# A decoder trunk on one core: chunk 3 of x1 on ScalarE, a unit's splits ahead of the second half's norm, and block 0 of the last norm on VectorE

## The chip, the core and the metric

The kernel runs on one core of a Trainium2 chip. A core has TensorE for matrix products (PE; its weight loads are shown as PEld), VectorE (DVE), ScalarE (ACT), GpSimd (POOL) and SyncE (SP), which here only issues transfers. Each engine works through its own list of instructions in order and waits on semaphores for the others. PE writes into PSUM; DVE and ACT read PSUM and SBUF. Transfers between HBM and SBUF run on 16 DMA engines, whoever issues them.

The metric is device time in microseconds (us) of one execution; lower is better. The kernel before took 1002.99 us, the median of three runs (1001.86 to 1003.0).

## The reference

The input is a sequence of 256 tokens of width 2048. Two layers follow, each closed by `x <- LayerNorm(alpha * x + mixer(x))`, in float32:

- a Mamba-2 SSD mixer (input projection 2048 to 10304, a short convolution, the chunked state-space product, a gate, a group norm, output projection 4096 to 2048);
- a sliding-window attention mixer with sinks (32 query heads, 4 key/value heads of 64). Keys and values come from the first layer's output by one shared projection of 2048 to 512; queries and gate come from another of 2048 to 4096; an output projection of 2048 to 2048 ends it.

What the change touches is the LayerNorm after the first layer, whose result is called x1 here, the K/V projection behind it, and the LayerNorm after the second layer, whose result is the output:

```
def _layernorm(x, g, b):
    mu = mean(x); var = mean((x - mu)^2)
    return (x - mu) * rsqrt(var + EPS) * g + b
kv = x1 @ kv_w + kv_b
```

## The kernel before

**Split products.** Every large product is made of three, to keep float32 accuracy: each operand is split into a high half (ACT copies it to a reduced float32, tile `wh` for weights, L158) and a low half (DVE subtracts the high half from the original, tile `wl`, L161), and PE adds high x high, low x high and high x low. x1 is split likewise into `x1H` (L893, one of them L891 on DVE) and `x1L` (L894).

**Units.** Weights come in units of 128 x 2048. `load_next` (L219) loads a unit as two 512 KB transfers on SP into the rotating raw tiles `wr` and splits both halves (`split_half`, L152). `next_unit` (L231) hands out the next unit and sees to it that two more are loaded behind it (`AHEAD = 2`). There are four buffers each of `wh` and `wl` and six of `wr`.

**Order.** The program order of each engine is set by a scheduler from dependences and priorities; instructions marked with `keep_in_program_order` (the arguments `pin`, `pin_h`, and the helper `ordered` in the last norm) keep the order in which the code writes them.

**Between the layers.** The rows are two halves (h) of 128 tokens; a chunk or block (c, nb) is 512 of the 2048 columns. L900 to L908 run the last output products of the first layer in the order (0,0), (1,0), (0,1), (0,2), (0,3), (1,1), (1,2), (1,3) of (h, nb), add the result to `xr` (L312) and take each block's statistics (L843). Behind a half's last block, `center(h)` (L860) makes mean (L847), scale `rs` (L849, L850, ACT) and `nmr` (L864), and centres and scales the half: chunks 0 and 2 on DVE (L870), 1 and 3 on ACT (L868). `turn_x1(h, c)` (L872) then transposes a chunk on PE (L877), applies the norm's g and b from PSUM in four pieces of 128 (even chunks on ACT, L887; odd ones on DVE, L885) and splits it.

**K/V.** L955 to L963: for h = 0, four units are taken one after the other; `x_stat` (L936) makes twelve matmuls of 512 columns for each (L944). The argument `last` puts one of the three products of a unit at its end. Behind the third unit, the four chunks of the second half are transposed. For h = 1 the same four units are used again.

**The last norm.** `out_last` (L316) makes the last output products, and `behind` (L1216) takes statistics; behind the last piece of the second half, `last` (L1194) runs. It makes mean and scale, a diagonal matrix `dg` of the scale on ACT (L1202), and centres the four blocks on DVE (`centre`, L1175, times g). Then some pieces get scale and bias on PE (identity x b, L1199, then `dg` x the centred piece, L1208) and are copied to `xr` by ACT (L1209); the others get them on DVE (`scale`, L1182). `store` (L1171) issues the output transfers, on SP unless another engine is named.

Of the kernel before, what the change touches and what calls it, by code (L numbers as in the profile page):

```python
# [27 lines left out]
AHEAD = 2  # L28
# [54 lines left out]
def trunk(ctx: ExitStack, tc: tile.TileContext, A: dict, out: bass.AP, dbg=None):  # L83
    nc = tc.nc
# [49 lines left out]
    WHOLE = [(0, 0, KT)]  # L134
# [17 lines left out]
    def split_half(u, raw, c, pin=False, pin_h=False):  # L152
        for (h, k0, k1), (l, _, _) in zip(*u.parts):
            a, b = max(k0, 8 * c), min(k1, 8 * c + 8)
            if a < b:
                sl = slice((a - k0) * P, (b - k0) * P)
                v = raw[:, (a - 8 * c) * P : (b - 8 * c) * P]
                m = nc.scalar.activation(h[:, sl], v, AF.Copy)  # L158
                if pin_h:
                    tc.keep_in_program_order(m)  # L160
                m = nc.vector.tensor_tensor(l[:, sl], v, h[:, sl].bitcast(F32), ALU.subtract)  # L161
                if pin:
                    tc.keep_in_program_order(m)

    def load_unit(src, places, pin=False):
        u = new_unit(places)
        raws = [load_half(u, src, c) for c in range(2)]
        for c in range(2):
            split_half(u, raws[c], c, pin, pin)
        return u  # L170

    def load_first():
# [24 lines left out]
    srcs = []  # L197
# [12 lines left out]
    places = {}  # L210
# [5 lines left out]
    units = []  # L216
    used = [0]

    def load_next(n, pin=False):  # L219
        for _ in range(n):  # L220
            if len(units) == 4:
                nc.sync.dma_start(cc[:], A["cc"])
            for i in [i for i, n in enumerate(XK_AT) if n == len(units)]:

                v = xr[:, i % 2, i // 2 * 1024 : i // 2 * 1024 + 1024]
                tc.keep_in_program_order(
                    nc.sync.dma_start(v, A["xk"][:, i % 2, i // 2 * 1024 : i // 2 * 1024 + 1024])
                )
            units.append(load_unit(srcs[len(units)], places.get(len(units), [WHOLE, WHOLE]), pin))

    def next_unit():  # L231
        load_next(min(used[0] + 1 + AHEAD, len(srcs)) - len(units))
        used[0] += 1
        return units[used[0] - 1]

# [29 lines left out]
    xr = xr_t[:, : 2 * D].rearrange("p (h d) -> p h d", h=2)  # L265
# [591 lines left out]
    nc.gpsimd.dma_start(gbc[:], A["gbc"])  # L857
    st1 = lp.tile([P, 2, 4, 6], F32, tag="st", name="st1")

    def center(h):  # L860

        mv, rs = norm_scale(lp, st1, h)
        nmr = lp.tile([P, 1], F32, tag="nmr", name=nm("nmr"), bufs=2)
        nc.vector.tensor_scalar(nmr[:], mv[:, 0:1], rs[:], -1.0, ALU.mult, ALU.mult)  # L864
        for c in range(4):
            v = xr[:, h, c * 512 : (c + 1) * 512]
            if c % 2:
                nc.scalar.activation(v, v, AF.Identity, scale=rs[:], bias=nmr[:])  # L868
            else:
                nc.vector.tensor_scalar(v, v, mv[:, 0:1], rs[:], ALU.subtract, ALU.mult)  # L870

    def turn_x1(h, c, tp, tag, bufs):  # L872

        ps = ax_tile()
        for k in range(4):
            pinned(
                nc.tensor.transpose(  # L877
                    ps[:, k * P : (k + 1) * P], xr[:, h, c * 512 + k * P : c * 512 + (k + 1) * P], ident
                ), True,
            )  # L880
        x1 = tp.tile([P, 512], F32, tag=tag, name=nm("x1"), bufs=bufs)[:].rearrange("p (k t) -> p k t", k=4)
        for k in range(4):
            v, g_, b_ = ps[:, k * P : (k + 1) * P], *[gbc[:, i, c * 4 + k : c * 4 + k + 1] for i in range(2)]
            if c % 2:
                nc.vector.tensor_scalar(x1[:, k, :], v, g_, b_, ALU.mult, ALU.add)  # L885
            else:
                nc.scalar.activation(x1[:, k, :], v, AF.Identity, scale=g_, bias=b_)  # L887
        dst = (slice(None), slice(c * 4, c * 4 + 4), slice(h * P, (h + 1) * P))
        if (h, c) == (0, 0):

            nc.vector.tensor_copy(x1H[dst], x1)  # L891
        else:
            nc.scalar.activation(x1H[dst], x1, AF.Copy)  # L893
        nc.vector.tensor_tensor(x1L[dst], x1, x1H[dst].bitcast(F32), ALU.subtract)  # L894
# [5 lines left out]
    for h, nb in ((0, 0), (1, 0), (0, 1), (0, 2), (0, 3), (1, 1), (1, 2), (1, 3)):  # L900
        if h == 0:
            us[nb] = next_unit()
        out_unit(*yHL, h, us[nb], nb, False, rms, True)
        norm_stats(st1, h, nb)
        if nb == 3:
            center(h)
        for c in {(1, 2): (0, 1), (1, 3): (2, 3)}.get((h, nb), ()):
            turn_x1(0, c, x1p, "x1", 2)  # L908
    s2.close()
# [26 lines left out]
    def x_stat(ps, h, u, ui, pin=False, last=None):  # L936

        todo = [(k, i) for k in range(4) for i in range(3) if i != last]
        todo += [(k, last) for k in range(4) if last]
        for k, i in todo:  # L940
            kk = ui * 4 + k
            ks = slice(k * 512, (k + 1) * 512)
            hs = slice(h * P, (h + 1) * P)
            m = nc.tensor.matmul(  # L944
                ps[:], (x1H, x1L, x1H)[i][:, kk, hs], (u.h, u.h, u.l)[i][:, ks],
                start=(kk, i) == (0, 0), stop=ui == 3 and (k, i) == todo[-1],
            )
            pinned(m, pin)
# [5 lines left out]
    kv_u = []  # L954
    for h in range(2):  # L955
        ps = mm_tile()
        for ui in range(4):
            if h == 0:
                kv_u.append(next_unit())
            x_stat(ps, h, kv_u[ui], ui, h == 0, (1, 1, 2, None)[ui] if h == 0 else None)  # L960
            if h == 0:
                for c in ((), (), (0, 1, 2, 3), ())[ui]:
                    turn_x1(1, c, bp, "pt", NPT)  # L963
        kd = bp.tile([P, 4, 2, 64], F32, tag="qt", name=nm("kd"), bufs=2)
        nc.vector.tensor_tensor(
            kd[:, :, 0, :], ps[:, :256].rearrange("p (j d) -> p j d", j=4),
            kvb[:, :256].rearrange("p (j d) -> p j d", j=4), ALU.add,
        )
        nc.vector.tensor_tensor(vt[:, h, :], ps[:, 256:], kvb[:, 256:], ALU.add)
        rope(kd[:, :, 0, :], h, 4)  # L970
        nc.gpsimd.tensor_copy(kd[:, :, 1, :], kd[:, :, 0, :])

        def ktr(h=h, kd=kd):
            pt = ax_tile()
            for j in range(4):
                nc.tensor.transpose(
                    pt[:, j * P : (j + 1) * P], kd[:, j, :, :].rearrange("p a d -> p (a d)"), ident
                )
            nc.scalar.copy(kT[:, :, h * P : (h + 1) * P], pt[:].rearrange("p (j t) -> p j t", j=4))

        later(2, ktr)
# [185 lines left out]
    def cols(nb, c0=0, c1=512):  # L1167
        return slice(nb * 512 + c0, nb * 512 + c1)

    def store(h, sl, eng=nc.sync):  # L1170
        ordered(eng.dma_start(out[h * P : (h + 1) * P, sl], xr[:, h, sl]))  # L1171

    def centre(h, nb):
        t = bp.tile([P, 512], F32, tag="pt", name=nm("t"), bufs=NPT)
        ordered(nc.vector.scalar_tensor_tensor(  # L1175
            t[:], xr[:, h, cols(nb)], sc[h][0][:, 0:1], gb2[0][:, cols(nb)], ALU.subtract, ALU.mult
        ))
        ts[h, nb] = t

    def scale(h, nb, c0=0):  # L1180
        sl = cols(nb, c0)
        ordered(nc.vector.scalar_tensor_tensor(  # L1182
            xr[:, h, sl], ts[h, nb][:, c0:], sc[h][1][:], gb2[1][:, sl], ALU.mult, ALU.add
        ))
        store(h, sl)
# [7 lines left out]

    def last():  # L1194

        pieces = [(0, 0, 256), (0, 256, 512), (1, 0, 512), (2, 0, 256)]
        pss = [ax_tile()[:, : p[2] - p[1]] for p in pieces]
        for p, ps in zip(pieces, pss):
            ordered(nc.tensor.matmul(ps, ident, gb2[1][:, cols(*p)], start=True, stop=False))  # L1199
        sc[1] = norm_scale(bp, st2, 1, 5)  # L1200
        dg = bp.tile([P, P], F32, tag="dg", name="dg")
        ordered(nc.scalar.activation(dg[:], ident, AF.Copy, scale=sc[1][1][:]))  # L1202
        for c in range(4):
            centre(1, c)
            for p, ps in zip(pieces, pss):
                if p[0] != c:
                    continue
                ordered(nc.tensor.matmul(ps, dg[:], ts[1, c][:, p[1] : p[2]], start=False, stop=True))  # L1208
                ordered(nc.scalar.copy(xr[:, 1, cols(*p)], ps))  # L1209
                if c == 0:  # L1210
                    store(1, cols(*p))
        scale(1, 3)
        scale(1, 2, 256)
        store(1, slice(512, 1280), nc.scalar)

    def behind(h, nb, c0=0, c1=512):  # L1216
        ordered(norm_stats(st2, h, nb, c0, c1))
# [105 lines left out]
```

## Time and profile before

| what | value |
|---|---|
| median of three runs | 1002.99 us (1001.86, 1002.99, 1003.0) |
| the profiled execution | 1002.04 us, its span 1000.2 us |
| PE busy | 992.7 us, 99% of the span |
| DVE, ACT, POOL busy | 772.9, 565.8, 105.2 us |
| HBM read | 195.43 MB |
| granted TensorE clock | 1.00 of full speed |

How the lines are read: times are in us from the start of the span unless marked ns. A row of the timeline has start, length, engine, line of the kernel, operation, destination <- source, shape, a count (xN, instructions of one kind merged into one row), and in brackets how long the engine was idle before it and what it waited for. A row of waits has: engine, line and what it waited for; then total us, number of times, longest. The chain of waits is the path that ended last, followed back from the last instruction. In the DMA view, a line of GB/s gives 40 equal slices of the window, and a row of issues gives the count, KB each, and the median us from issue to landing. The queue called q14 brings instructions.

### The profile page before, as it was taken

To read this page: it belongs to the slowest core of one execution; us is meant where nothing else is said; L and a number is where in the kernel's file an instruction comes from. 1 tells how busy PE (TensorE), PEld (TensorE's weight loads), DVE (VectorE), ACT (ScalarE), POOL (GpSimd) and SP (SyncE) were. 2 spreads that over 40 slices of the span, in tenths; PEclk is the share of its full clock that TensorE was granted. 3 is DMA by queue.
4 is the path that set the end of the run, shared out by engine and by line. 5 is a ranking of instruction groups with operands and counts; after the bars stand their busy time and mean duration, and the time that the engine had idled before them with its cause. 6 is when DMAs were issued, how large, how long until landed. Compare 5 with 4: busy or idle time off the path is not lost.

```text
span 1000.2 us, 17847 instructions
## 1 busy us (share of the span) xinstructions
PE 992.7 (99%) x7040; PEld 900.3 (90%) x7040; DVE 772.9 (77%) x1189; ACT 565.8 (57%) x986; POOL 105.2 (11%) x130
## 2 busy tenths in 40 slices
PE   9999999999999999999999999999999999999997
PEld 8999989999999998999999999888988878878976
DVE  7888897867886886786786787898688775775685
ACT  7595856547746645664654764565545544544632
POOL 0001303004003003000300300303000000000003
PEclk9999999999999999999999999999999999999999
DMA  9798587565576655666656556457654546546422
GB/s 358 251 285 296 169 273 211 175 226 177 183 242 183 224 195 191 213 193 207 206 174 225 164 177 223 163 162 252 230 194 148 182 147 195 159 149 194 167 104 84
DMA packets 58963, 198.81 MB, mean 199 GB/s; under 512 B 6560, under 2 KB 10944, under 8 KB 58624
## 3 DMA queue, kind: packets, MB, share of 16 engines
q1 hardware_dynamic: 56080, 188.47, 57.8%
q0 software_dynamic: 2336, 8.69, 2.7%
q8 instruction: 55, 0.90, 0.4%
q10 hardware_dynamic: 464, 0.52, 0.1%
q14 instruction: 28, 0.23, 0.1%
HBM read 195.43 MB, written 2.23 MB: 198 GB/s over the span
## 4 chain that ended last, share of the span: by engine, by line
PE 96%; DVE 2%; ACT 1%; issue 0%; DVEq 0%; ACTq 0%
PE mm L238 52%; PE mm L944 10%; PE mm L305 9%; PE mm L307 8%; PE mm L306 8%; PE ax L605 2%; PE ax L1056 1%; PE ax L1114 1%; PE ax L581 1%; PE ax L1096 1%; ACT wh L158 1%; DVE wl L161 0%; PE mm L364 0%; PE ax L564 0%; PE ax L1019 0%
## 5 line engine op out<-in xcount | busy, mean ns | idle before, releaser
L161 DVE TENSOR_TENSOR wl<-wr,wh 128x1024 fp32r<-128x1024 f32 (+2 forms) x338 | 393.0, 1182 | 109.0 <-ACT wh L158 106.7
L158 ACT ACTIVATE wh<-wr 128x1024 fp32r<-128x1024 f32 (+2 forms) x338 | 332.7, 1011 | 208.4 <-issue 84.9
L238 PE MATMUL mm<-xH,wh 128*128 128x256 f32 x1280 | 356.0, 278 | 0.0
L238 PE MATMUL mm<-xL,wh 128*128 128x256 f32 x1280 | 354.4, 277 | 0.0
L238 PE MATMUL mm<-xH,wl 128*128 128x256 f32 x1280 | 354.3, 277 | 0.0
L238 PEld LDWEIGHTS mm<-xH,wh 128*128 128x128 f32 x1280 | 240.9, 188 | 2.1 <-issue 0.5
L238 PEld LDWEIGHTS mm<-xL,wh 128*128 128x128 f32 x1280 | 240.9, 188 | 1.0
L238 PEld LDWEIGHTS mm<-xH,wl 128*128 128x128 f32 x1280 | 240.9, 188 | 0.0
L305 PE MATMUL mm<-wh,yH 128*128 128x512 f32 x256 | 101.4, 396 | 0.0
L306 PE MATMUL mm<-wh,yL 128*128 128x512 f32 x256 | 99.8, 390 | 0.0
L307 PE MATMUL mm<-wl,yH 128*128 128x512 f32 x256 | 99.7, 389 | 0.0
L621 POOL TENSOR_TENSOR yz<-yz,z 128x256 f32<-128x256 f32 x32 | 32.8, 1032 | 472.2 <-DVE yz L616 472.2
L238 PE MATMUL mm<-x1H,wh 128*128 128x256 f32 x256 | 71.7, 280 | 0.0
L468 DVE SCALAR_TENSOR_TENSOR cv<-mm,pc,cv 128x255 f32<-128x255 f32 x144 | 68.5, 476 | 3.3 <-ACT cv L466 1.9
L238 PE MATMUL mm<-x1L,wh 128*128 128x256 f32 x256 | 70.8, 277 | 0.0
L238 PE MATMUL mm<-x1H,wl 128*128 128x256 f32 x256 | 70.8, 276 | 0.0
L944 PE MATMUL mm<-wh,x1H 128*128 128x512 f32 x160 | 62.9, 393 | 0.0
L944 PE MATMUL mm<-wl,x1H 128*128 128x512 f32 x160 | 62.1, 390 | 0.6 <-DVE wl L161 0.6
L944 PE MATMUL mm<-wh,x1L 128*128 128x512 f32 x160 | 61.3, 389 | 0.0
L305 PEld LDWEIGHTS mm<-wh,yH 128*128 128x128 f32 x256 | 48.1, 188 | 10.3 <-DVE z L557 1.0
L307 PEld LDWEIGHTS mm<-wl,yH 128*128 128x128 f32 x256 | 48.1, 188 | 10.2
L312 DVE SCALAR_TENSOR_TENSOR xr<-mm,r,xr 128x512 f32<-128x512 f32 x64 | 47.0, 743 | 12.0 <-PE mm L307 7.7
(210 smaller groups left out, 1349.7 us busy)
## 6 DMA issues: line engine op xcount, KB each, us to landing
wr<-in_wa SPq DMA_DIRECT2D x154, 512.0 KB, 4.9
wr<-in_wo SPq DMA_DIRECT2D x64, 512.0 KB, 4.4
wr<-in_wq SPq DMA_DIRECT2D x32, 512.0 KB, 4.8
wr<-in_wg SPq DMA_DIRECT2D x32, 512.0 KB, 4.7
wr<-in_wb SPq DMA_DIRECT2D x32, 512.0 KB, 4.5
rb<-rscr SPq DMA_DIRECT2D x11, 512.0 KB, 4.2
wr<-in_wkv SPq DMA_DIRECT2D x8, 512.0 KB, 5.0
first<-in_first SPq DMA_DIRECT2D x11, 352.0 KB, 6.4
```

The source lines that it names most:

```text
L158: m = nc.scalar.activation(h[:, sl], v, AF.Copy)
L161: m = nc.vector.tensor_tensor(l[:, sl], v, h[:, sl].bitcast(F32), ALU.subtract)
L238: m = nc.tensor.matmul(ps, a, b, start=first and i == 0, stop=last and i == 2)
L305: pinned(nc.tensor.matmul(ps, aH[:, k, hs], u.h[:, ks], start=k == 0, stop=False), pin)
L306: pinned(nc.tensor.matmul(ps, aL[:, k, hs], u.h[:, ks], start=False, stop=False), pin)
L307: pinned(nc.tensor.matmul(ps, aH[:, k, hs], u.l[:, ks], start=False, stop=k == 3), pin)
L312: nc.vector.scalar_tensor_tensor(v, ps, rms[:, h : h + 1], v, ALU.mult, ALU.add)
L468: nc.vector.scalar_tensor_tensor(a[:, sft:], ps[:, : S - sft], w(3 - sft), a[:, sft:], ALU.mult, ALU.add)
L581: nc.tensor.transpose(ps[:, o : o + P], st.xs[i][:, c * P : (c + 1) * P], ident)
L605: nc.tensor.matmul(ps[64 * r : 64 * r + 64, cols], xd[:, c, r, :], e[:, 256:] if c else e[:, :256], start=c == 0, stop=c == 1,)
L621: nc.gpsimd.tensor_tensor(v, v, st.z[i][:], ALU.mult)
L944: m = nc.tensor.matmul(ps[:], (x1H, x1L, x1H)[i][:, kk, hs], (u.h, u.h, u.l)[i][:, ks], start=(kk, i) == (0, 0), stop=ui == 3 and (k, i) = ...
```

## The change

1. In `turn_x1`, chunk 3 of the first half gets g and b on ACT in place of DVE.
2. `center` is divided: `center_scale` makes mean, scale and nmr; `center` does the centring. For the second half the centring is called in the K/V loop, behind the first `next_unit`, which loads the third K/V unit. The `next_unit` at ui = 1, which loads the fourth, pins the low halves' splits of its unit in program order (`pin`), not the high halves' (`pin_h`). In the compiled order on DVE, the second low half of the third unit and the low part of chunk 3 stand ahead of the second half's nmr and centring.
3. The first K/V unit of the second half multiplies by the low x (x1L) last.
4. In the last norm, DVE scales block 0 behind the second centring; blocks 1 and 2 take scale and bias on PE, block 2 in two pieces of 256; DVE scales block 3. The second half goes out in four transfers of 256 KB, three on SP and block 2's on ACT, in place of five.

```diff
-    def load_unit(src, places, pin=False):
+    def load_unit(src, places, pin=False, pin_h=False):
         u = new_unit(places)
         raws = [load_half(u, src, c) for c in range(2)]
         for c in range(2):
-            split_half(u, raws[c], c, pin, pin)
+            split_half(u, raws[c], c, pin, pin_h)
         return u
...
-    def load_next(n, pin=False):
+    def load_next(n, pin=False, pin_h=True):
...
-            units.append(load_unit(srcs[len(units)], places.get(len(units), [WHOLE, WHOLE]), pin))
-
-    def next_unit():
-        load_next(min(used[0] + 1 + AHEAD, len(srcs)) - len(units))
+            units.append(load_unit(srcs[len(units)], places.get(len(units), [WHOLE, WHOLE]), pin, pin and pin_h))
+
+    def next_unit(behind=False):
+        load_next(min(used[0] + 1 + AHEAD, len(srcs)) - len(units), behind, not behind)
         used[0] += 1
         return units[used[0] - 1]
...
-    def center(h):
-
+    def center_scale(h):
         mv, rs = norm_scale(lp, st1, h)
         nmr = lp.tile([P, 1], F32, tag="nmr", name=nm("nmr"), bufs=2)
         nc.vector.tensor_scalar(nmr[:], mv[:, 0:1], rs[:], -1.0, ALU.mult, ALU.mult)
+        return mv, rs, nmr
+
+    def center(h, mv, rs, nmr):
+
         for c in range(4):
...
-            if c % 2:
+            if c % 2 and (h, c) != (0, 3):
                 nc.vector.tensor_scalar(x1[:, k, :], v, g_, b_, ALU.mult, ALU.add)
...
         if nb == 3:
-            center(h)
+            scale1 = center_scale(h)
+            if h == 0:
+                center(h, *scale1)
...
             if h == 0:
-                kv_u.append(next_unit())
-            x_stat(ps, h, kv_u[ui], ui, h == 0, (1, 1, 2, None)[ui] if h == 0 else None)
+
+                kv_u.append(next_unit(ui == 1))
+                if ui == 0:
+                    center(1, *scale1)
+            x_stat(ps, h, kv_u[ui], ui, h == 0, ((1, 1, 2, None), (1, None, None, None))[h][ui])
...
-        pieces = [(0, 0, 256), (0, 256, 512), (1, 0, 512), (2, 0, 256)]
+        pieces = [(1, 0, 512), (2, 0, 256), (2, 256, 512)]
...
         for c in range(4):
             centre(1, c)
+            if c == 1:
+                scale(1, 0)
             for p, ps in zip(pieces, pss):
-                if p[0] != c:
-                    continue
-                ordered(nc.tensor.matmul(ps, dg[:], ts[1, c][:, p[1] : p[2]], start=False, stop=True))
-                ordered(nc.scalar.copy(xr[:, 1, cols(*p)], ps))
-                if c == 0:
-                    store(1, cols(*p))
+                if p[0] == c:
+                    ordered(nc.tensor.matmul(ps, dg[:], ts[1, c][:, p[1] : p[2]], start=False, stop=True))
+                    ordered(nc.scalar.copy(xr[:, 1, cols(*p)], ps))
+            if c in (1, 2):
+                store(1, cols(c), nc.sync if c == 1 else nc.scalar)
         scale(1, 3)
-        scale(1, 2, 256)
-        store(1, slice(512, 1280), nc.scalar)
```

## The prediction

> **What bounds the kernel.** I read the page first (busy time, the chain), then what PE waited for, then the timeline of PE, DVE and ACT around the one long wait, then the last 15 us with the DMA view.
>
> ```profile
> span 1000.2 us, 17847 instructions
> PE 992.7 (99%) x7040; PEld 900.3 (90%) x7040; DVE 772.9 (77%) x1189; ACT 565.8 (57%) x986; POOL 105.2 (11%) x130
> PE 96%; DVE 2%; ACT 1%; issue 0%; DVEq 0%; ACTq 0%
> ...
> PE ax L350 <- DVE zero L339: 1.2, 1, 1.2
> PE mm L944 <- DVE wl L161: 0.6, 1, 0.6
> ```
>
> PE is busy for 99% of the span and is 96% of the chain that ended last, so time can only leave where PE stands still or after its last matmul. The waits of PE have two rows: the start of the kernel (untouched), and one wait of a K/V matmul for a low half made on DVE. The other stretch off PE is the end, which the chain walks on DVE. The change edits exactly these two places.
>
> The place of the wait, from the timelines of PE, DVE and ACT:
>
> ```profile
> 669.22 0.39 PE L944 MATMUL mm<-wh,x1H 128*128 128x512 f32 x1
> 669.45 0.39 PE L944 MATMUL mm<-wh,x1L 128*128 128x512 f32 x1
> 671.03 0.61 PE L944 MATMUL mm<-wl,x1H 128*128 128x512 f32 x2
> 672.27 0.73 PE L944 MATMUL mm<-wl,x1H 128*128 128x512 f32 x2 [0.62 <-DVE wl L161]
> 672.84 1.91 PE L877 MATMUL ax<-cc,xr 128*128 128x128 f32 x16
> 674.50 0.48 PE L944 MATMUL mm<-wh,x1H 128*128 128x512 f32 x1
> ...
> 668.46 0.26 DVE L847 BATCH_NORM_AGGREGATE mv<-st 128x2 f32<-128x24 f32 x1
> 668.64 0.66 DVE L885 TENSOR_SCALAR x<-ax,gbc 128x128 f32<-128x128 f32 x2
> 669.32 0.21 DVE L864 TENSOR_SCALAR nmr<-mv,rs 128x1 f32<-128x1 f32 x1
> 669.45 1.00 DVE L870 TENSOR_SCALAR xr<-xr,mv,rs 128x512 f32<-128x512 f32 x2
> 670.36 0.73 DVE L885 TENSOR_SCALAR x<-ax,gbc 128x128 f32<-128x128 f32 x2
> 671.00 1.22 DVE L161 TENSOR_TENSOR wl<-wr,wh 128x1024 fp32r<-128x1024 f32 x1
> 672.13 0.69 DVE L894 TENSOR_TENSOR x1L<-x,x1H 128x512 fp32r<-128x512 f32 x1
> 672.73 2.36 DVE L161 TENSOR_TENSOR wl<-wr,wh 128x1024 fp32r<-128x1024 f32 x2
> ...
> 665.66 1.50 ACT L887 ACTIVATE x<-ax,gbc 128x128 f32<-128x128 f32 x4
> 667.19 0.63 ACT L893 ACTIVATE x1H<-x 128x512 fp32r<-128x512 f32 x1
> 668.75 0.29 ACT L849 ACTIVATE rs<-mv,eps_t 128x1 f32<-128x1 f32 x1 [0.93 <-DVE mv L847]
> 669.57 1.52 ACT L868 ACTIVATE xr<-xr,nmr,rs 128x512 f32<-128x512 f32 x2 [0.28 <-DVE nmr L864]
> 671.12 0.63 ACT L893 ACTIVATE x1H<-x 128x512 fp32r<-128x512 f32 x1
> ```
>
> DVE holds the second low half of the third K/V unit (671.00) behind seven small operations that began at 668.64. PE starts a 512-column matmul every 0.23 us (669.22, 669.45), so the second pair, begun at 672.27, was due at 671.03 + 0.46 = 671.49, and the transposes, begun at 672.84, at 671.03 + 4 x 0.23 = 671.95. The wait is 0.62 us by its own row, 0.78 from start to start, 0.89 at the transposes.
>
> **The change, part by part.**
>
> *The fourth chunk on ScalarE, and the third unit's splits ahead of the norm.* Only the order moves here; the scaling of chunk 3 of the first half (four L885 on DVE) becomes four L887 on ACT, and the compiled order on DVE is now: mean (L847), second low half of the third unit, low part of chunk 3, nmr, two centrings, the fourth unit's two low halves. SP's and POOL's queues keep their order in this stage, so no load moves past another.
> - The low half: starts at 668.64 in place of 671.00 and is done at 668.64 + 1.22 = 669.86, while PE asks for it at 671.49: 1.6 us to spare. The wait goes.
> - ACT: the four scalings follow the row at 667.19, at 667.72 to 669.2 (1.50 by the row at 665.66). The two small steps of the scale now come at 669.1 and, with chunk 3's high part (0.63) between them, at 669.95 to 670.15 instead of ending about 669.28. Behind them waits DVE's nmr.
> - DVE: low part of chunk 3 after its high part, 670.1 to 670.8; nmr 670.7; centrings 670.8 to 671.8. ACT's two centrings: 670.95 to 672.47 (1.52).
> - What is late next: the norm is 1.4 us later, and the transposes of the second half come 0.89 us earlier. Chunk 0 is asked for at 671.95 (ready 671.4), chunk 1 at 672.37 (ready 671.75), chunk 3 at 671.95 + 12 x 0.104 = 673.2 (ready 672.47; 0.104 is the start-to-start 1.66 us of sixteen, 672.84 to 674.50). The least slack is 0.7 us. The fourth unit's low halves run 671.8 to 674.1; PE asks for the first at 674.1 and for the second at 675.5, so 1.2 us to spare.
>
> The new order costs nothing of its own as long as that 0.7 us holds; without it each us of delay is one on PE. Bounds of this edit: a gain of 0.62 (the row of the wait) to 0.89 (start to start at the transposes). I take 0.85, as starts are what moves the end.
>
> The row says that one scaling is 0.37 us on ACT (1.50 for four) against 0.34 on DVE (0.73 for two is 0.37, 1.36 for four is 0.34, below). The Trainium skill, "ScalarE: Activation LUTs", Rules for kernel authors, speaks against the move: multiplies and adds belong on VectorE, not on ScalarE. Here the rows differ by about 0.1 us over the four, and ACT has the time, so by the rule the edit would lose 0.1 us, by the trace nothing.
>
> *The second half's first unit multiplied by the low x last* (x_stat with last = 1 for h = 1): twelve matmuls in another order, none added. Its need of chunk 0's low part moves from the second matmul to the ninth.
>
> ```profile
> 675.01 0.63 ACT L893 ACTIVATE x1H<-x 128x512 fp32r<-128x512 f32 x1
> 675.68 0.69 DVE L894 TENSOR_TENSOR x1L<-x,x1H 128x512 fp32r<-128x512 f32 x1 [0.27 <-ACT x1H L893]
> 676.29 1.36 DVE L885 TENSOR_SCALAR x<-ax,gbc 128x128 f32<-128x128 f32 x4
> ...
> 741.87 0.68 DVE L1107 COPY pt<-ax 128x512 f32<-128x512 f32 x1
> 742.61 1.53 PE ax L1056 x8
> ```
>
> PE reaches that place 2.74 us after the fourth unit's start, before at 677.2, now at 676.35; chunk 0's high part is done at 674.9 by the new ACT order and its low part at 676.1, against a need at 678.2. Cost zero; cover gone, at most 0.1 us. Later, in the attention, PE waits about 0.5 us for a DVE copy (741.87, 742.61). A PE that comes 0.85 us earlier could wait there longer: the loss lies between nothing and 0.85. DVE's work there is released by matmuls and by freed buffers, which come earlier too, so I take nothing.
>
> *The last norm.* Before, ACT took blocks 0, 1 and half of 2 through PE, DVE block 3 and the other half; after, DVE scales block 0 behind two centrings, ACT takes 1 and 2, DVE block 3. Four output transfers instead of five (rows of DVE, ACT, SP and the DMA views):
>
> ```profile
> 991.43 2.74 DVE L1175 SCALAR_TENSOR_TENSOR t<-xr,mv,gb 128x512 f32<-128x512 f32 x4
> 994.27 1.15 DVE L1182 SCALAR_TENSOR_TENSOR xr<-t,rs,gb 128x512 f32<-128x512 f32 x2
> 994.47 0.86 ACT L1209 COPY xr<-ax 128x512 f32<-128x512 f32 x2 [0.49 <-PE ax L1208]
> 995.36 0.38 ACTq L1171 DMA_DIRECT2D out<-xr  x1
> 993.58 2.54 SPq L1171 DMA_DIRECT2D out<-xr  x4
> ...
> GB/s 0 0 0 146 424 410 366 410 425 497 373 395 373 439 351 344 380 234 37 29 29 15 0 0 0 0 0 0 0 0 0 0 0 0 0 0 0 0 0 0
> q14 instruction: 1, 0.01, 0.6%
> out<-xr ACTq DMA_DIRECT2D x1, 384.0 KB, 3.6
> out<-xr SPq DMA_DIRECT2D x1, 128.0 KB, 3.3
> ...
> out<-xr SPq DMA_DIRECT2D x4, 256.0 KB, 2.0
> ```
>
> DVE: four centrings at a step of 0.66 and a scaling put third: 991.43, 992.09, 992.76 (scaling of block 0), 993.42, 994.09, then, with the 0.1 us that the row at 994.27 shows behind the operation it depends on, 994.94 to 995.69. It ended at 994.27 + 1.15 = 995.42, so DVE is 0.27 later. ACT: block 2's centring ends at 994.17 in place of 993.50, its products and two copies follow, and the last copy ends about 995.68 in place of 995.33. So both last transfers are ready at 995.7. Before, ACT's went out at 995.36 and SP's, ready at 995.42, only at 993.58 + 2.54 - 0.33 = 995.78, right behind it; now the second goes at about 996.08.
>
> Bytes: the last two were 384 + 128 KB behind a 256 KB one sent when block 3 was scaled, at 994.27 + 0.75 = 995.02; they become 256 + 256 KB, with the 256 KB ahead of them sent at about 994.6 and gone. The GB/s row (slices of 0.14 us) shows traffic from 995.8 to 997.95 at about 390 GB/s. After: 512 KB from 996.55 at that rate end at 997.95. The two orders come out even, within 0.2 us.
>
> But in the row of before the last 0.55 us run at 15 to 37 GB/s: one of sixteen DMA engines is late, in a window that also holds one instruction load (q14). The last landed at 995.78 + 3.3 = 999.1; without the thin part it would have been about 998.5. After, SP has two instructions fewer before this point (a transfer and its wait). If the load still falls on the last transfers the end stays within 0.1 of 999.1; if not, 0.6 is saved. Two instructions of SP are one issue, 0.4 to 1 us, and the last transfers run for 1.4 us, so the load more likely falls on them again than not: I take a gain of 0.1, with bounds of a gain of 0.6 and a loss of 0.3 (DVE's 0.27 passed on in full).
>
> **Sum.** 0.85 + 0 + 0.10 = 0.95 us. The profiled execution took 1002.04 us (span 1000.2 and 1.84 around it): 1001.1. The three runs had 1001.86, 1002.99 and 1003.0, their median 0.95 above the profiled one, so the same sum on the median gives 1002.04; I predict the middle, 1001.5. No change can be told from 0.2%, about 2.0 us.
>
> **Rivals.**
> - *The instruction load leaves the transfers.* A further 0.5 us: 1001.0, and with the half us at the L1056 wait going too, 1000.5, or 1000.1 on the profiled execution's footing; this is where "faster" by over 2.0 us lies. For it: the thin part is 0.55 us long and two instructions fewer move the load. Against: the shift is shorter than the transfers. The Trainium skill, "Runtime: NRT & Kernel Launch", Instruction fetch mechanics, has refills bound to the place in the instruction stream, at block ends, which is this mechanism; only the rate of the one late engine bears on it here.
> - *The gain is swallowed at L1056.* If DVE's queue there doesn't come earlier, PE loses the 0.85 at 742: 1002.4. For it: PE does wait there for DVE's copy. Against: that copy's input is PE's own product.
> - *ScalarE is late (the other side).* ACT runs in order, and the norm now stands behind chunk 3's scalings and its high part. If these run d later than worked out, chunk 3's transposes stall by d - 0.7; from d = 1.6 the stall removed is paid back, and each us beyond is lost. Slower than the median by 2.0 us (1005.0) takes d = 0.7 + 0.85 + 2.6 = 4.2. Against: the products that the scalings read are made before 669.22, and ACT stood idle for 0.93 at 668.75.
>
> **Chances.** Forecast 0.58, the load leaves 0.25, swallowed 0.10, ScalarE late 0.07. Nearly all of the second case and a little of the first pass the 2.0 us below the median: faster 0.28; slower only the last: 0.07; the rest 0.65. Range: 1000.1 (load gone, on the lower footing) to 1002.8 (swallowed, on the median's).
>
> **What would show it.** Right: no PE wait for wl at L944, transposes 0.9 us earlier, the low half at about 668.6; last DVE scaling ending 0.27 later in its stage, two 256 KB transfers within 0.4 us of each other and the last landing as far behind the first centring as before (999.1 - 991.43 = 7.7 us). Wrong: a PE wait for xr or x1H at the transposes or in the second half; a longer wait at L1056; a final GB/s row without the thin tail.

## The result, and the profile after

| what | before | after |
|---|---|---|
| median of 22 executions each, same chips | 1001.73 us (1001.24 to 1003.48) | 1000.5 us (1000.05 to 1001.26) |
| ratio after to before, 95% interval | | 0.9985 [0.9979, 0.9992] |
| the profiled execution, and its span | 1002.04, 1000.2 us | 1000.24, 998.3 us |
| first K/V matmul to the transposes of the second half | 9.16 us | 8.27 us |
| first K/V matmul to the mean of the last norm | 327.42 us | 326.53 us |
| mean of the last norm to the start of the span's last instruction, 0.05 us ahead of its end | 9.00 us | 8.61 us |

The change saves 1.23 us on the medians. The interval excludes 1, but 0.15% lies within the 0.2% that the prediction called the same. The two profiled executions also differ by 0.53 us before the K/V stage begins (663.68 and 663.15 below), where the change edits nothing; so what follows compares distances inside a stage, and not times from the start of the span.

The page of the kernel after (head, chain) and the waits of PE:

```profile
span 998.3 us, 17836 instructions
PE 991.3 (99%) x7036; PEld 898.9 (90%) x7036; DVE 771.9 (77%) x1185; ACT 566.5 (57%) x989; POOL 105.3 (11%) x130
PE 98%; DVE 1%; issue 0%; ACT 0%; DVEq 0%
...
PE ax L350 <- DVE zero L339: 1.2, 1, 1.2
PE ax L1217 <- DVE t L1183: 1.1, 1, 1.1
```

PE's wait for a low half is gone. The new row at L1217 stands in the last norm, where PE waits for a centred block before its last products; before, these took block 0 first, and no such row stands in the list. The lines have moved: L944 is now L949, L864 is L863, L868 is L871, L870 is L873, L877 is L880, L885 is L888, L887 is L890, L893 is L896, L894 is L897, and in the last norm L1175 is L1183, L1182 is L1190, L1208 is L1217, L1209 is L1218, L1171 is L1179.

The start of the K/V stage before, from the timeline of PE, and then the same place after, from the timelines of PE, DVE and ACT:

```profile
663.68 0.48 PE L944 MATMUL mm<-wh,x1H 128*128 128x512 f32 x1
```

```profile
663.15 0.48 PE L949 MATMUL mm<-wh,x1H 128*128 128x512 f32 x1
...
670.50 1.07 PE L949 MATMUL mm<-wl,x1H 128*128 128x512 f32 x4
671.42 1.91 PE L880 MATMUL ax<-cc,xr 128*128 128x128 f32 x16
...
667.93 0.26 DVE L847 BATCH_NORM_AGGREGATE mv<-st 128x2 f32<-128x24 f32 x1
668.11 1.16 DVE L161 TENSOR_TENSOR wl<-wr,wh 128x1024 fp32r<-128x1024 f32 x1
669.42 0.69 DVE L897 TENSOR_TENSOR x1L<-x,x1H 128x512 fp32r<-128x512 f32 x1 [0.15 <-ACT x1H L896]
670.03 0.21 DVE L863 TENSOR_SCALAR nmr<-mv,rs 128x1 f32<-128x1 f32 x1
670.15 0.99 DVE L873 TENSOR_SCALAR xr<-xr,mv,rs 128x512 f32<-128x512 f32 x2
671.06 2.35 DVE L161 TENSOR_TENSOR wl<-wr,wh 128x1024 fp32r<-128x1024 f32 x2
...
667.20 1.49 ACT L890 ACTIVATE x<-ax,gbc 128x128 f32<-128x128 f32 x4
668.57 0.30 ACT L849 ACTIVATE rs<-mv,eps_t 128x1 f32<-128x1 f32 x1
670.27 1.53 ACT L871 ACTIVATE xr<-xr,nmr,rs 128x512 f32<-128x512 f32 x2 [0.80 <-DVE nmr L863]
```

The four matmuls with the low half run as one row without a break, and the transposes start 671.42 - 663.15 = 8.27 us behind the first K/V matmul instead of 672.84 - 663.68 = 9.16. The low half is split right behind the mean. The order on DVE is the one in the prediction; nmr comes 2.1 us behind the mean.

The last norm after, from the timelines of DVE, ACT and SP, and the DMA view of the last 4.9 us (slices of 0.12 us):

```profile
989.68 0.29 DVE L847 BATCH_NORM_AGGREGATE mv<-st 128x2 f32<-128x30 f32 x1
...
993.44 0.75 DVE L1190 SCALAR_TENSOR_TENSOR xr<-t,rs,gb 128x512 f32<-128x512 f32 x1
993.53 0.80 ACT L1218 COPY xr<-ax 128x256 f32<-128x256 f32 x2 [0.24 <-PE ax L1217]
994.37 0.38 ACTq L1179 DMA_DIRECT2D out<-xr  x1
989.20 5.35 SPq L1179 DMA_DIRECT2D out<-xr  x4
...
GB/s 351 17 0 0 0 234 401 435 385 451 218 17 117 334 435 368 451 385 402 401 385 418 385 184 17 67 0 0 0 0 0 0 0 0 0 0 0 0 0 0
q14 instruction: 1, 0.01, 0.4%
out<-xr SPq DMA_DIRECT2D x2, 256.0 KB, 2.0
out<-xr ACTq DMA_DIRECT2D x1, 256.0 KB, 2.8
```

The last DVE scaling ends at 994.19, 4.51 us behind the mean (before: 991.10 to 995.42, 4.32, the mean's row is quoted with the experiments). The last SP transfer is issued at 989.20 + 5.35 - 0.33 = 994.22 and ACT's at 994.37. The instruction load is still in the window, but the thin tail of the GB/s row is two slices, 0.25 us, where the row of before had four slices of 0.14 us, 0.55 us. A transfer lands in sixteen parts. By the landing times in the traces, the last part of all comes 7.50 us behind the mean (before: 8.02), and 0.25 us behind the part of the same transfer that landed just ahead of it (before: 0.67).

### The profile page after: what moved, and what is told of

The parts are those of the page before. It is cut to its first block, busy times and chain, and to the rows that moved or that the text cites. A ratio compares the mean times of both kernels' runs of the same rounds, so it can differ in the third digit from the quotient of the medians.

```text
span 998.3 us, 17836 instructions
## 1 busy us (share of the span) xinstructions
PE 991.3 (99%) x7036; PEld 898.9 (90%) x7036; DVE 771.9 (77%) x1185; ACT 566.5 (57%) x989; POOL 105.3 (11%) x130
## 4 chain that ended last, share of the span: by engine, by line
PE 98%; DVE 1%; issue 0%; ACT 0%; DVEq 0%
PE mm L238 52%; PE mm L949 10%; PE mm L305 9%; PE mm L306 9%; PE mm L307 9%; PE ax L605 2%; PE ax L1064 1%; PE ax L1122 1%; PE ax L581 1%; PE ax L1104 1%; PE mm L364 0%; PE ax L564 0%; PE ax L1027 0%; PE ax L880 0%; PE ax L350 0%
## 5 line engine op out<-in xcount | busy, mean ns | idle before, releaser
L949 PE MATMUL mm<-wh,x1H 128*128 128x512 f32 x160 | 62.9, 393 | 0.0
L949 PE MATMUL mm<-wl,x1H 128*128 128x512 f32 x160 | 61.8, 389 | 0.0
L949 PE MATMUL mm<-wh,x1L 128*128 128x512 f32 x160 | 60.9, 390 | 0.0
```

The lines of the kernel that those rows point to most:

```text
L949: m = nc.tensor.matmul(ps[:], (x1H, x1L, x1H)[i][:, kk, hs], (u.h, u.h, u.l)[i][:, ks], start=(kk, i) == (0, 0), stop=ui == 3 and (k, i) = ...
```

## The experiments

Three things were to be told apart. First, whether the 0.9 us at the K/V matmuls comes from the low half's place alone, whether the scaling on ScalarE is needed for it, and whether it reaches the end. Second, whether the gain at the end comes from the new order of the last norm or from the place of the instruction load. Third, how much slack the transposes have, since the prediction's slower case hung on it. In the table, "stage" is the distance from the first K/V matmul to the mean of the last norm, "end" the distance from that mean to the start of the last instruction (0.05 us ahead of the end of the span), and "load" the start of the instruction load behind that mean (all us, from the profiled executions); the ratio is that of the timed executions.

| run | median (before beside it) | ratio | stage | end | load |
|---|---|---|---|---|---|
| before | 1001.73 | | 327.42 | 9.00 | 5.58 |
| after | 1000.5 (1001.73) | 0.9985 [0.9979, 0.9992] | 326.53 | 8.61 | 6.92 |
| e1_between | 1000.79 (1001.78) | 0.9992 [0.9984, 1.0001] | 326.49 | 9.10 | 5.57 |
| e2_tail | 1001.52 (1001.78) | 0.9996 [0.9987, 1.0005] | 327.43 | 8.60 | 6.91 |
| e3_c3dve | 1000.78 (1001.78) | 0.9987 [0.9978, 0.9996] | 326.70 | 8.60 | 6.91 |
| e4_c3act | 1000.88 (1001.78) | 0.9991 [0.9982, 1.0] | 326.51 | 9.07 | 5.56 |
| e9_nopin | 1001.06 (1001.82) | 0.9991 [0.9982, 1.0] | 326.83 | 8.60 | 6.92 |
| e7_rs5 | 1000.64 (1001.82) | 0.999 [0.998, 0.9999] | 326.57 | 8.62 | 6.93 |
| e7_rs12 | 1002.62 (1001.73) | 1.0009 [1.0, 1.0018] | 328.06 | 8.61 | 6.92 |
| f1_after_sp2 | 1005.71 (1001.82) | 1.0041 [1.0026, 1.0056] | 331.53 | 8.66 | 5.17 |
| f2_before_sp8 | 1000.79 (1001.82) | 0.9991 [0.9982, 1.0] | 327.44 | 8.31 | -1.51 |
| g1_after_sp8 | 1000.03 (1001.73) | 0.9982 [0.9973, 0.9991] | 326.49 | 8.32 | -1.53 |
| g2_best | 1000.12 (1001.73) | 0.9983 [0.9975, 0.9992] | 326.53 | 8.31 | -1.52 |
| g4_pad64 | 1004.87 (1001.73) | 1.0031 [1.0019, 1.0043] | 331.48 | 8.60 | 6.92 |

Medians that differ by some tenths of a us are not told apart by themselves (the intervals are about 0.9 us to each side); the distances are, since kernels with the same code in a stage agree there within 0.1 us (f1 and g4 apart, whose tiles lie at other addresses). In runs that add lines of code, the line numbers lie two or three above those of the kernel they start from.

**The two halves of the change, each alone.** e1 is the changed kernel with the last norm of before:

```diff
-        pieces = [(1, 0, 512), (2, 0, 256), (2, 256, 512)]
+        pieces = [(0, 0, 256), (0, 256, 512), (1, 0, 512), (2, 0, 256)]
...
-            if c == 1:
-                scale(1, 0)
...
         scale(1, 3)
+        scale(1, 2, 256)
+        store(1, slice(512, 1280), nc.scalar)
```

> The changes between the two layers alone, with the last norm of before. My theory (two separate gains: 0.9 us from the K/V wait, 0.5 us at the end, where the changed kernel's instruction load no longer falls on the last transfers): the PE wait for wl at L949 is gone, and the time from the first K/V matmul to the last mean of the second norm is 0.9 us shorter; from that mean to the end it stays 9.0 us as in before. In all 0.9 us faster (ratio 0.9991). Rival (the whole gain comes from the stage between the layers, the end only varies from run to run): 1.3 to 1.5 us faster, with the end's distance anywhere between 8.6 and 9.0.

e2 is the kernel before with the last norm of after (the same lines the other way):

> The last norm of after alone, all else as before. My theory: the PE wait at L944 stays (0.8 us from start to start), the end comes 8.6 us behind the last mean in place of 9.0, and the instruction load starts about 6.9 us behind that mean, after the last data: 0.4 to 0.5 us faster (ratio 0.9995). Rival (the end only varies): no difference, 9.0 us behind the mean.

e1 keeps the whole stage gain, 327.42 - 326.49 = 0.93, and none at the end (9.10). e2 has nothing of the first and all of the second: 8.60. The medians are 0.99 and 0.26 lower than before, together 1.25, against 1.23 for the whole change; with intervals this wide so close a match is luck, and the distances say the same more firmly: 0.93 and 0.40, against 0.89 and 0.39 in the changed kernel. Before, and then e1: the mean of the last norm (timeline of DVE), and for e1 the DMA view of its last 5 us (slices of 0.125 us):

```profile
991.10 0.29 DVE L847 BATCH_NORM_AGGREGATE mv<-st 128x2 f32<-128x30 f32 x1
```

```profile
989.41 0.29 DVE L847 BATCH_NORM_AGGREGATE mv<-st 128x2 f32<-128x30 f32 x1
...
GB/s 0 0 0 0 351 368 435 385 418 410 493 401 376 376 376 401 401 293 401 334 109 33 33 8 25 33 17 8 0 0 0 0 0 0 0 0 0 0 0 0
q14 instruction: 1, 0.01, 1.0%
```

With the last norm of before, the load falls on the last transfers again and the thin tail is back: seven slices, 0.9 us, at 8 to 33 GB/s where sixteen engines move some 400, the rate of about one engine (400 / 16 = 25).

**Which line of the stage's edit does it.** e3 is the changed kernel with chunk 3 on DVE as before:

```diff
-            if c % 2 and (h, c) != (0, 3):
+            if c % 2:
```

> The changed kernel with chunk 3 of the first half scaled on DVE as before, the splits still ahead of the centring. My theory (it is enough that the third unit's second low half starts 2.8 us or less behind the mean): the compiled order puts that low half behind four scalings and nmr, so it starts 1.5 us behind the mean in place of 2.5 (before) and -0.1 to 0.2 (after), ends just ahead of PE's need, and nearly all the gain stays: a PE wait of at most 0.2 us there, 1.2 to 1.4 us faster than before in all. Rival (ScalarE's taking of chunk 3 is what frees DVE): half or more of the wait is back, at least 0.4 us, and the whole is at most 0.9 us faster.

e4 is the kernel before with that one line of the change:

```diff
-            if c % 2:
+            if c % 2 and (h, c) != (0, 3):
```

> Before with one line changed: chunk 3 of the first half scaled on ACT. The compiled order on DVE then has the third unit's second low half right behind the mean, with no pinning and no division of the centring. My theory: the PE wait for wl is gone and 0.9 us with it, from the first K/V matmul on; the end stays 9.0 us behind the last mean. Rival (the pinned order of the splits is needed): a wait at the transposes or at the fourth unit of 0.3 us or more takes its place, since nmr and the centrings now stand behind two low halves.

Timelines of e3 (DVE, PE), and then of e4 (DVE):

```profile
668.58 0.26 DVE L847 BATCH_NORM_AGGREGATE mv<-st 128x2 f32<-128x24 f32 x1
668.76 0.66 DVE L888 TENSOR_SCALAR x<-ax,gbc 128x128 f32<-128x128 f32 x2
...
670.21 1.22 DVE L161 TENSOR_TENSOR wl<-wr,wh 128x1024 fp32r<-128x1024 f32 x1
...
672.40 0.54 DVE L873 TENSOR_SCALAR xr<-xr,mv,rs 128x512 f32<-128x512 f32 x1
...
671.14 1.09 PE L949 MATMUL mm<-wl,x1H 128*128 128x512 f32 x4
672.07 2.02 PE L880 MATMUL ax<-cc,xr 128*128 128x128 f32 x16
```

```profile
667.93 0.26 DVE L847 BATCH_NORM_AGGREGATE mv<-st 128x2 f32<-128x24 f32 x1
668.11 2.29 DVE L161 TENSOR_TENSOR wl<-wr,wh 128x1024 fp32r<-128x1024 f32 x2
670.31 0.21 DVE L864 TENSOR_SCALAR nmr<-mv,rs 128x1 f32<-128x1 f32 x1
```

In e3 the split order alone puts the low half at 670.21, 1.6 us behind the mean where it was 2.5 before (668.46 to 671.00); PE no longer waits for it, and the transposes start 672.07 - 663.79 = 8.28 us behind the first K/V matmul, as in the changed kernel (8.27). The stage is still 0.17 us longer (326.70 against 326.53). Of this, 0.11 is lost inside the transposes, which take 2.02 us in place of 1.91: the second centring, of chunk 2, ends at 672.94, just when PE comes to that chunk. In e4 the one line alone gives all of it (326.51): with four scalings fewer on DVE, the scheduler itself puts two low halves right behind the mean. So either edit removes the wait. The one line is enough, and beside it the divided centring, the pin and the low x multiplied last add nothing that the stage shows.

The pinning of the fourth unit, taken out of the changed kernel (e9):

```diff
-                kv_u.append(next_unit(ui == 1))
+                kv_u.append(next_unit())
```

> The changed kernel without the pinning of the fourth unit's low halves: in the compiled order on DVE the fourth unit's first low half then stands ahead of nmr, and the centrings come about 1.1 us later. My theory (slack of 0.7 to 0.9 us at the transposes): PE waits at most 0.4 us there, so 0 to 0.4 us slower than the changed kernel. Rival (pinning matters in full): 1.1 us slower.

The timelines of DVE and PE of e9:

```profile
667.77 0.26 DVE L847 BATCH_NORM_AGGREGATE mv<-st 128x2 f32<-128x24 f32 x1
667.95 2.29 DVE L161 TENSOR_TENSOR wl<-wr,wh 128x1024 fp32r<-128x1024 f32 x2
670.15 0.21 DVE L863 TENSOR_SCALAR nmr<-mv,rs 128x1 f32<-128x1 f32 x1
...
670.32 1.07 PE L949 MATMUL mm<-wl,x1H 128*128 128x512 f32 x4
671.47 1.97 PE L880 MATMUL ax<-cc,xr 128*128 128x128 f32 x16
```

A low half of the fourth unit goes ahead of nmr, and the transposes start 1.15 us behind the row of four instead of 0.92 (670.50 to 671.42). The stage is 0.30 longer. With the centring divided, the pin is worth that; the median agrees in sign and doesn't show it by itself. Without the divided centring it isn't needed: e4 has neither and loses nothing.

**How much slack the transposes have.** Five, and then twelve, copies of the scale onto itself on ACT ahead of nmr, which change no value:

```diff
         mv, rs = norm_scale(lp, st1, h)
+        for _ in range(5 if h else 0):
+            nc.scalar.copy(rs[:], rs[:])
```

> The changed kernel with five more copies of the second half's scale onto itself on ACT (128x1, each waiting for the one before), ahead of nmr: about 1.6 us of delay for nmr and the centrings, with no other engine loaded. My theory (the transposes of the second half have 0.7 to 0.9 us of slack): PE waits 0.7 to 0.9 us there, at chunk 0, 1 or 3, and the kernel is 0.7 to 0.9 us slower than the changed one, so 0.5 us faster than before. Rival (the slack is larger, the norm is far off the path): no new wait. Other rival (no slack): 1.6 us slower.

> The changed kernel with twelve copies of the scale onto itself on ACT ahead of nmr, at 0.22 us each as in the run with five: nmr about 2.1 us later than in the changed kernel. With five copies nmr came 0.6 us later and PE didn't wait. My theory (slack 0.9 us at chunk 3's transposes, 0.6 or so at chunk 0's): PE waits 1.2 to 1.6 us at the transposes. Rival (the norm is far off the path): no wait.

The five copies missed what was expected of them: nmr came 2.71 us behind the mean (667.83 to 670.54) in place of 2.10, only 0.6 later, because part of the copies filled time in which DVE was making the low part of chunk 3 anyway; PE waited for nothing, and the transposes start 8.25 us behind the first K/V matmul, so the slack is no less than about 0.6. The twelve go beyond it (PE's waits, the timelines of ACT, DVE, PE):

```profile
PE ax L882 <- DVE xr L875: 1.3, 1, 1.3
...
670.10 2.65 ACT L863 COPY rs<-rs 128x1 f32<-128x1 f32 x12
...
668.52 0.26 DVE L847 BATCH_NORM_AGGREGATE mv<-st 128x2 f32<-128x24 f32 x1
...
672.78 0.21 DVE L865 TENSOR_SCALAR nmr<-mv,rs 128x1 f32<-128x1 f32 x1 [2.08 <-ACT rs L863]
...
671.09 1.07 PE L951 MATMUL mm<-wl,x1H 128*128 128x512 f32 x4
673.50 1.20 PE L882 MATMUL ax<-cc,xr 128*128 128x128 f32 x9 [1.34 <-DVE xr L875]
```

nmr is 4.26 behind the mean, 2.16 later than in the changed kernel. The transposes start 2.41 us behind the row of four in place of 0.92, so 1.49 is lost, and the stage is 1.53 longer. If each us beyond the slack is one of PE's, the slack is 2.16 - 1.5 = 0.66 us, which fits the five copies. The median is 2.12 above the changed kernel's, of which 1.53 is accounted for by the stage; the rest is within what the intervals leave open.

**Whose the end is.** Small transfers on SP of 4 KB each, whose data nobody reads, move everything that SP issues later by as many instructions. Two of them in the changed kernel:

```diff
     def load_next(n, pin=False, pin_h=True):
...
+            if 30 <= len(units) < 32:
+                jk = cst.tile([P, 8], F32, tag=f"jk{len(units)}", name=nm("jk"))
+                nc.sync.dma_start(jk[:], A["inv"])
```

> The changed kernel with two more small transfers (4 KB each) on SP, at the loads of units 30 and 31, whose data nothing reads: they bring SP's instruction list back to the length of before ahead of the last transfers. My theory (an instruction load of SP, bound to a place in its list, falls on the last transfers in before and behind them in after): the load again starts about 5.6 us behind the last mean, one DMA engine is late by about 0.5 us, and the end comes 9.0 us behind the mean in place of 8.6: 0.4 us slower than the changed kernel. Rival (the four equal transfers and their order make the end shorter): the end stays 8.6 us behind the mean. Third (the load belongs to another engine): its start doesn't move with SP's count.

Eight in the kernel before (`< 38`):

> Before with eight more small transfers (4 KB each) on SP, one at each of the loads of units 30 to 37, whose data nothing reads: SP's list is some eight or nine instructions longer ahead of the last transfers. My theory: the instruction load comes earlier, before the last two transfers (2 to 4 us behind the last mean), no DMA engine is late at the end, and the end comes 8.4 us behind the mean in place of 9.0, so 0.5 us faster than before with the last norm unchanged. Rival: the end stays 9.0 us behind the mean.

f1 missed. The load did come earlier, 5.17 instead of 6.92, while the last transfers run, and one engine was late again (the last landing came 0.51 us behind the one before it, and 7.68 behind the mean where the changed kernel has 7.50), but the end took 8.66, not 9.0, and 5 us were lost in the stage, which is taken up below. So of the 0.39 us that the changed kernel gains at the end, putting the load back on its last transfers takes away only 0.05. f2 moves the load out of the end altogether, to 1.51 us ahead of the mean. The DMA view of its last 4.9 us has no row for q14 and no thin tail, and the last landing comes 0.01 us behind the one before it:

```profile
GB/s 368 226 100 351 385 234 9 0 0 0 134 451 351 351 418 393 494 451 426 401 309 451 418 426 334 335 260 17 0 0 0 0 0 0 0 0 0 0 0 0
out<-xr ACTq DMA_DIRECT2D x1, 384.0 KB, 2.9
```

ACT's 384 KB land in 2.9 us instead of 3.6, and the end takes 8.31: the last norm of before, without the load, is 0.3 us shorter than the last norm of after with the load at 6.92. So the same eight in the changed kernel, and in the kernel with the edit of the stage and the last norm of before:

> The changed kernel with the eight small transfers on SP (units 30 to 37), so that the instruction load comes well before the last transfers. My theory (the two last norms take the same time, and only the load tells them apart): the load starts before the last mean or less than 3 us behind it, no DMA engine is late, the last landing is 7.2 us behind the mean in place of 7.5, the end 8.2 to 8.3: 0.3 us faster than the changed kernel. Rival (the new order of the last norm has its own share): the end comes at 8.0 or earlier, 0.3 us or more ahead of the 8.3 of before with eight transfers.

> The changes between the layers with the last norm of before and the eight small transfers on SP. My theory: from the first K/V matmul to the last mean 326.5 us (as in the changed kernel), the end 8.3 us behind it; 0.9 + 0.7 = 1.6 us faster than before, 0.2 to 0.3 us faster than the changed kernel, though the last norm is the old one. Rival (the new last norm is needed): no faster than the changed kernel.

Both end in 8.3 us (8.32 and 8.31). With the load away the two last norms take the same time, so the new one gains nothing of its own: it gains only where a load is near. With one, the old norm pays 0.69 us (9.00 against 8.31) and the new one 0.29 (8.61 against 8.32, load at 6.92) or 0.34 (8.66, load at 5.17). So the later place of the load is not shown to be the whole of the 0.39; f1's load starts 0.4 us earlier than that of before, and why the new norm loses so little to it is open. Both kernels are the fastest here, 0.4 to 0.5 us below the changed one by their medians, but the intervals don't separate them from it. That the load belongs to SP is inferred from this: its place moves where the number of SP's instructions changes (e1, e2, f1, f2, g1, g2) and stays where only other engines' lists are edited (e3, e7, e9 and g4 against after, e4 against before).

**The 5 us of f1.** Its two tiles of 32 bytes move all later tiles by 64 bytes. The changed kernel with an unused tile of 64 bytes and no transfers:

```diff
+    jk = cst.tile([P, 16], F32, tag="jk", name="jk")
+    nc.gpsimd.memset(jk[:], 0.0)
```

> The changed kernel with one unused tile of 64 bytes per partition among the constants, set once by GpSimd, and no more transfers: every later tile lies 64 bytes further. Theory (the changed kernel with two small transfers lost 5 us because its two 32-byte tiles moved the others by 64 bytes, and PE then starts the gate products' matmuls every 118 to 123 ns in place of 114 to 118): about 5 us slower than the changed kernel, from the first K/V matmul to the last mean 331.5 in place of 326.5, the end unchanged at 8.6. Rival (the two transfers themselves, or the load that they move, cost it): no difference.

The stage takes 331.48, as in f1 (331.53). The gate products' rows by line, after and then here, with the shortest, median and longest duration in ns and the first and last start:

```profile
L238 PE MATMUL mm<-x1H,wh x256: 276/276/385, 709.4 to 939.8; 128*128 128x256 f32 x128
L238 PE MATMUL mm<-x1L,wh x256: 276/276/285, 709.5 to 939.9; 128*128 128x256 f32 x128
```

```profile
L240 PE MATMUL mm<-x1H,wh x256: 279/282/385, 709.1 to 944.0; 128*128 128x256 f32 x128
L240 PE MATMUL mm<-x1L,wh x256: 274/281/287, 709.3 to 944.1; 128*128 128x256 f32 x128
```

The same matmuls stretch over 234.9 us instead of 230.4: 4.5 of the 5 us, spread over all of them. PE's list of waits has no row for it, and the granted clock is 1.00 in this window in both runs. Most of these matmuls start 115 to 122 ns apart, where they start 113 or 114 ns apart in the changed kernel (the expectation's 114 to 118 was too high). f1 has the transfers and no memset, g4 the memset and no transfers; both have the 64 bytes. The eight tiles of f2, g1 and g2 (256 bytes) cost nothing. Why 64 bytes do is not settled.

## Why the prediction was right, point by point

- *The sum.* Forecast 0.95 us off the kernel before, measured 1.23 on the medians. The time itself, 1001.5, stood on the first three executions and on the profiled one; the median of before over 22 is 1001.73, and 0.95 off that is 1000.8 against 1000.5. It was partly luck that "the same" came out: against the 1002.99 from which the prediction counted, 1000.5 is 2.5 us less and would have passed its 2.0. By the distances the two terms measured 0.89 and 0.39, where 0.85 and 0.10 were forecast. The range's upper end should have read 1002.9 (1002.04 + 0.85).
- *The low half and the transposes (0.85 taken of 0.62 to 0.89).* Right, and the size by starts was the right one to take: 0.89 at the transposes and 0.89 at the mean of the last norm. The order on DVE and ACT was as worked out; nmr came 2.1 us behind the mean where 670.7 against 668.46 had said 2.24.
- *The low x multiplied last.* Cost zero, as forecast, and of no use here either: e4 keeps the old order and its stage is as short (326.51).
- *The 0.7 us of slack.* 0.66 by e7_rs12. The step named chunk 3 for it, though its own numbers gave chunk 0 less (671.95 against 671.4, 0.55); the wait that came was for a chunk that DVE centres (row L882 <- DVE xr L875), at the first of the transposes, so chunk 0 binds.
- *ScalarE in place of DVE.* The Trainium skill, "ScalarE: Activation LUTs", Rules for kernel authors, sends multiplies and adds to VectorE. The four scalings took 1.49 us on ACT (row at 667.20) against 1.36 on DVE (row at 676.29), so the rule agrees in the price of the work and not in the time: e3, which follows it, is 0.17 us longer in the stage, since with the four scalings on DVE the second centring comes only just in time.
- *The gain swallowed at the copy wait.* Wrong as a rival, as the prediction held: 0.89 at the transposes is 0.89 at the last mean.
- *ScalarE late.* The mechanism exists and was not reached: the one delay measured beyond the slack, 2.16 us, cost the stage 1.53.
- *The last norm.* DVE's scaling is 0.19 later, not 0.27. The second of the last transfers was forecast about 0.4 us behind the first (996.08 against 995.7); they are issued 0.15 apart. "The two orders come out even, within 0.2 us" holds to 0.01 with the load away (8.32 and 8.31).
- *The instruction load.* This is the step that was mis-sized: "the load more likely falls on them again than not: I take a gain of 0.1". It forecast the last landing as far behind the first centring as before, 7.7 us; it came at 7.2 (7.50 behind the mean, the centring 0.33). A final row without the thin tail was to speak against it, and the row of after has two slices of it left. The load moved from 5.58 to 6.92 us behind the mean, to the end of the data, and the end came 0.39 us earlier. So the case that was given 0.25 is nearer to what happened, though 0.39 is less than its 0.1 + 0.5, and f1 shows that the load's place is not all of it. The step took the shift as one issue, 0.4 to 1 us; it was 1.34, and what sets the load's start is not shown. The Trainium skill, "Runtime: NRT & Kernel Launch", Instruction fetch mechanics, calls the cost of crossing a block of instructions mostly hidden; here it is hidden where it meets no transfer that the end waits for (f2, g1) and costs 0.7 us in before, where it does (9.00 against 8.31 in f2).

What kept the forecast right is that this term and the others together stay under 0.2%. The two cases, forecast and "the load leaves", lay 0.5 us apart, less than a measurement of this kernel tells.

## What to carry to other kernels

Size a wait of the busiest engine by its loss in starts at the next work, not by its own row: here 0.89 us against 0.62, and with PE 96% of the chain all of it reached the last norm. When the end of a kernel gains some tenths of a us by an edit of its last transfers, look whether an instruction load falls on them: a few dummy transfers on the issuing queue, in both kernels, move the load away and show what the edit gains without it. An edit that seems to need several parts may need one: try each alone, as e4 did. A control that adds a tile moves the addresses of all later ones, so it needs a control of its own.

## What the runs showed of the hardware that was not expected

- 64 bytes of unused SBUF per partition ahead of the other tiles lengthened the kernel by 4.4 us on the median (1004.87 against 1000.5), 3.6 times what the whole change gained: 256-column matmuls took 281 to 282 ns in the median in place of 276, while 256 bytes cost nothing.
- An instruction load of about 0.01 MB, by its moves one of SP's, holds back one of sixteen DMA engines: with it on the last transfers, the last of sixteen landings came 0.67 us behind the one before it and ACT's 384 KB took 3.6 us to land; with it away, 0.01 and 2.9.
